# Weight sums of six output projection steps made in the mixer and kept in DRAM, and four instead of three pairs of each column group multiplied by sums

## The chip, the cores and the metric

The kernel runs on one core of one Trainium2 chip. The metric is the device time of one execution in microseconds (us), as the median of several runs. All times of single instructions come from one profiled execution. The engines are called PE (TensorE, matrix products), ACT (ScalarE), DVE (VectorE), POOL (GpSimd) and SP (SyncE, which here only issues transfers).

## The reference, cut to what matters

One layer of a streaming encoder: a gated linear attention mixer, an MLP with squared ReLU, and a last norm, on 256 tokens of width 2048, all in float32.

```python
def _gla_mixer(h, w_in, w_gate_up, b_gate, o_norm, w_out):
    proj = h @ w_in                                   # q, k, v, r and the gate's low rank
    ...                                               # chunked gated attention gives o
    o = o * lax.rsqrt(jnp.mean(o * o, axis=-1, keepdims=True) + EPS) * o_norm
    return (o * jax.nn.silu(r)) @ w_out               # the output projection, 2048 x 2048

def _sq_relu_mlp(h, w_up, w_down):
    a = jax.nn.relu(h @ w_up)
    return (a * a) @ w_down

h = x + _gla_mixer(_rmsnorm(x, gla_norm), ...)
h = h + _sq_relu_mlp(_rmsnorm(h, mlp_norm), w_up, w_down)
return _rmsnorm(h, final_norm)
```

The change touches the output projection, `(o * silu(r)) @ w_out`, and work that is put beside an earlier projection.

## The kernel before

**Precision.** Every float32 operand of a product is split into a high part (a copy in the type fp32r, made by ACT in `copy_hi`, L118) and a low part (the rest, made by DVE, L131). A product is then three: high by high, high by low, low by high. A weight tile goes DRAM to `raw` (six buffers, loaded by SP), from `raw` into a pair of tiles `hi` and `lo` (five buffers each, taken by `slots`), and from there to PE. Buffers rotate: a new tile waits until the last reader of the one five (or six) before it is done. So loads and splits run ahead of PE as far as the buffers let them.

**Order of the program.** The mixer runs first: projections for v (first half), k, q, v (second half, L551 and after), r (two halves), each as sixteen steps of 128 rows of the weight (`natural`, L176, and `turned`, L219). Between two steps `pump` takes one piece of side work (the gate, decays, scores L523, attention) from the queue `side`. Then comes the output projection in four column groups of 512 (`out_group`), then the MLP (L867 and after), whose loads of the up projection follow the last group in SP's stream. A scheduler fixes the order of instructions on every engine when the kernel is built; `issue_after` adds orders by hand.

**The output projection.** A group has eight steps, one for each pair `kp` of 128-row blocks of the weight. A *plain* step splits the 2 x 512 columns of its raw tile and multiplies them in 24 matmuls of 256 columns (four blocks of a 2 x 2 product, three terms, two column halves). A step *by sums* treats the pair as a 2 x 2 block product and does it with seven block products instead of eight, 21 matmuls, at the price of sums of weight blocks and of activation blocks. Its work:

- SP loads the two halves (256 KB each, L743) and POOL adds one block onto another with an accumulating transfer of 128 KB (L744);
- ACT and DVE split the three blocks that need no more sums (768 columns) and PE does three of the products (9 matmuls);
- DVE makes the other sums (`weight_sums`, L604 and L605), ACT copies the high parts (two copies of 512), DVE the low part (L773, 1024 columns), and PE does the other four products (12 matmuls). This second half is `pending`: it comes one step later.

Products by sums of the activation go into two extra banks, `sums_banks` (p16 and p57). After the last step by sums of a group ACT copies them out (L779, L780), DVE combines them (L781 to L784) and adds them to the plain banks into h (L787). The same two banks serve the next group.

**Activations.** `turn` transposes the gated output `on` (in group 0, L627) or finished columns of h (in groups 1 to 3, for the MLP), ACT and DVE split them (L640, L641). For the pairs in `FORMED` the split is `turn_pair`: ACT copies, DVE makes the sums of activation blocks (`form_sums`, L617), ACT and DVE split all eight forms (L618, L619). Before, `FORMED` is (0, 1, 7) and the order of the steps is (3, 0, 2, 1, 4, 7, 5, 6) in every group.

## Time and profile before

| | before |
|---|---|
| median of 3 runs | 1044.37 us (1044.07 to 1044.48) |
| the profiled execution | 1043.33 us, span 1041.5 us |
| mean granted clock of PE | 0.999 |
| PE, DVE, ACT, POOL busy | 99%, 83%, 71%, 11% of the span |
| DMA | 226.79 MB, mean 218 GB/s |

The span is what the profiler saw from the first to the last instruction; the execution's own time holds some 2 us more. A busy share is an average over stages; which engine waits for which is read from the chain of work that ended last and from the rows of single stages.

### The profile page before, as it was taken

The page shows a single profiled execution, that of the slowest core. Times are in us where ns is not written, and L with a number is a line of the kernel's source. Part 1 is how long each engine was busy: PE and PEld are TensorE (multiplying, and loading weights), DVE is VectorE, ACT ScalarE, POOL GpSimd, SP SyncE. Part 2 cuts the span into 40 slices and gives each one's busy share as a digit, 9 for nine tenths or more (in the row PEclk, how much of TensorE's full clock was granted, in tenths as well). Part 3 has the DMA queues.
Part 4 walks back from the last instruction along what each step waited for, and adds up shares of the span by engine and source line. Part 5 has one row for each costly group of instructions (what it writes and reads, how often), then busy time and mean ns, then how long its engine had stood idle before and what let it go on. Part 6 is the DMA issues. An engine that isn't in the chain of part 4 may idle for free.

```text
span 1041.5 us, 23180 instructions
## 1 busy us (share of the span) xinstructions
PE 1033.2 (99%) x9058; PEld 1032.8 (99%) x9058; DVE 865.3 (83%) x1171; ACT 736.9 (71%) x1088; POOL 119.5 (11%) x163
## 2 busy tenths in 40 slices
PE   9999999999999999999999999999999999999997
PEld 9999999999999999999999999999999999999997
DVE  6668654657599876989999999999999999999887
ACT  7685544546477665677778788778778778778685
POOL 0000000010111101111111121111111121111100
PEclk9999999999999999999999999999999999999999
DMA  9957664655667687678887887887888888887772
GB/s 341 338 164 220 189 199 144 181 145 180 194 182 210 206 263 197 175 207 239 224 249 226 230 233 227 233 243 214 253 227 225 245 228 228 237 233 219 234 243 86
DMA packets 119453, 226.79 MB, mean 218 GB/s; under 512 B 10752, under 2 KB 27904, under 8 KB 119216
## 3 DMA queue, kind: packets, MB, share of 16 engines
q1 hardware_dynamic: 100768, 207.46, 63.2%
q0 software_dynamic: 17856, 16.26, 10.3%
q10 hardware_dynamic: 720, 1.60, 0.4%
q8 instruction: 71, 1.16, 0.4%
q14 instruction: 38, 0.31, 0.1%
HBM read 223.17 MB, written 2.10 MB: 216 GB/s over the span
## 4 chain that ended last, share of the span: by engine, by line
PE 99%; issue 0%; ACT 0%; DVE 0%; POOLq 0%; POOL 0%; DVEq 0%
PE up L867 33%; PE acc L867 28%; PE acc L176 19%; PE acc L725 8%; PE acc L219 6%; PE aux L219 2%; PE aux L176 1%; PE aux L627 1%; PE aux L523 1%; PE aux L252 0%; ACT sqf L1206 0%; PE acc L424 0%; DVE hf L1278 0%; POOLq L1315 0%; POOL rf L358 0%
## 5 line engine op out<-in xcount | busy, mean ns | idle before, releaser
L118 ACT CAST hi<-raw 128x512 fp32r<-128x512 f32 (+4 forms) x634 | 512.0, 834 | 234.8 <-PE acc L176 69.0
L131 DVE TENSOR_TENSOR lo<-raw,hi 128x768 fp32r<-128x768 f32 (+3 forms) x226 | 238.0, 1057 | 100.1 <-ACT hi L118 97.4
L867 PE MATMUL acc<-hi,act 128*128 128x256 f32 x1696 | 247.7, 276 | 0.0
L867 PE MATMUL up<-hh,hi 128*128 128x256 f32 x1024 | 238.7, 276 | 0.0
L867 PE MATMUL up<-hl,hi 128*128 128x256 f32 x1024 | 238.7, 276 | 0.0
L165 DVE TENSOR_TENSOR lo<-raw,hi 128x1024 fp32r<-128x1024 f32 x160 | 194.7, 1219 | 28.3 <-ACT hi L118 26.3
L867 PEld LDWEIGHTS acc<-hi,act 128*128 128x128 f32 x1696 | 217.6, 188 | 0.0
L867 PEld LDWEIGHTS up<-hl,hi 128*128 128x128 f32 x1024 | 192.2, 188 | 0.0
L867 PEld LDWEIGHTS up<-hh,hi 128*128 128x128 f32 x1024 | 192.2, 188 | 0.0
L1077 POOL DMA_DIRECT2D raw<-in_w_down x112 | 97.1, 867 | 516.1 <-DMA raw<-in_w_down 231.0
L1137 DVE TENSOR_TENSOR lo<-raw,hi 128x1024 fp32r<-128x1024 f32 x112 | 136.4, 1218 | 1.1 <-ACT hi L118 1.1
L867 PE MATMUL up<-hh,lo 128*128 128x256 f32 x1024 | 137.0, 276 | 0.0
L867 PE MATMUL acc<-lo,act 128*128 128x256 f32 x848 | 133.8, 276 | 0.0
L867 PEld LDWEIGHTS up<-hh,lo 128*128 128x128 f32 x1024 | 125.7, 188 | 0.0
L867 PEld LDWEIGHTS acc<-lo,act 128*128 128x128 f32 x848 | 113.4, 188 | 0.0
L176 PE MATMUL acc<-hi,xA 128*128 128x256 f32 (+1 forms) x736 | 105.6, 278 | 0.0
L176 PEld LDWEIGHTS acc<-hi,xA 128*128 128x128 f32 x736 | 94.4, 188 | 0.0
L605 DVE TENSOR_TENSOR raw<-raw 128x512 f32<-128x512 f32 x124 | 85.6, 690 | 3.2
L176 PE MATMUL acc<-lo,xA 128*128 128x256 f32 (+1 forms) x368 | 61.5, 278 | 0.0
L604 DVE TENSOR_TENSOR raw<-raw 128x256 f32<-128x256 f32 x124 | 52.4, 423 | 2.9
L176 PEld LDWEIGHTS acc<-lo,xA 128*128 128x128 f32 x368 | 50.8, 188 | 0.2 <-DVE lo L131 0.2
L219 PE MATMUL acc<-xA,hi 128*128 128x256 f32 x288 | 49.2, 276 | 0.0
(181 smaller groups left out, 1220.0 us busy)
## 6 DMA issues: line engine op xcount, KB each, us to landing
raw<-in_w_up SPq DMA_DIRECT2D x128, 512.0 KB, 4.6
raw<-in_w_down SPq DMA_DIRECT2D x224, 256.0 KB, 4.3
raw<-in_w_in SPq DMA_DIRECT2D x80, 512.0 KB, 3.8
raw<-in_w_down POOLq DMA_DIRECT2D x112, 128.0 KB, 5.0
raw<-in_w_out SPq DMA_DIRECT2D x20, 512.0 KB, 4.9
raw<-in_w_down SPq DMA_DIRECT2D x16, 512.0 KB, 5.0
raw<-in_w_vg SPq DMA_DIRECT2D x14, 520.0 KB, 8.1
raw<-in_w_out SPq DMA_DIRECT2D x24, 256.0 KB, 3.5
```

Of the source, the lines that this page charges most:

```text
L118: last_hi[0] = nc.scalar.copy(to, raw)
L131: last_lo[0] = nc.vector.tensor_tensor(lo[:, s], raw[:, s], hi[:, s].bitcast(F32), op=ALU.subtract)
L165: last_lo[0] = nc.vector.tensor_tensor(to[1], dst, to[0].bitcast(F32), op=ALU.subtract)
L176: nc.tensor.matmul(o[:, m], x, w[:, m], start=first and c == 0, stop=last, skip_group_check=True)
L219: nc.tensor.matmul(o, u[:, i, s], m, start=kt == 0 and n == 0 and j % 2 == 0, stop=kt == KT - 1 and n == 2, skip_group_check=True,)
L523: nc.tensor.matmul(o, kab[:, k[0], c0 + c, k[1] : k[1] + P], q(qt[:, c0 + c]), start=c == 0, stop=c == 1)
L604: nc.vector.tensor_tensor(u[:, 2], u[:, 0], u[:, 2], op=ALU.subtract)
L605: return nc.vector.tensor_tensor(u[:, 1::2], u[:, 1::2], u[:, 2:3].to_broadcast([P, 2, T]), op=ALU.subtract)
L725: newest[0] = nc.tensor.matmul(bank[:, o + d : o + d + T], x, w[:, d : d + T], start=bank in sums_banks and bank.name not in begun, stop=l ...
L867: newest[0] = nc.tensor.matmul(o, x, w, start=first, stop=last, skip_group_check=True).ins
L1077: nc.gpsimd.dma_start(out=raw[:, :T], in_=src[:, 0, T:], accum_op=ALU.add)
L1137: last_lo[0] = nc.vector.tensor_tensor(to[1][:, :G], u, to[0][:, :G].bitcast(F32), op=ALU.subtract)
```

## The change

Six steps of the output projection, pairs 1 and 6 in column groups 1, 2 and 3, get the sums of their weights made ahead. `make_sums` gives two jobs for each: `high` takes a raw tile and a pair of high/low tiles, loads the 512 KB of the pair (SP), makes all sums on DVE (three instructions: a block added, then the two of `weight_sums`), copies the high part (ACT) and stores it to a tile in DRAM (POOL's queue); `low` makes the low part (DVE) and stores it too. `pump` now takes one job after its side work; the jobs come in threes (high, low, nothing), eighteen in all, from the second v projection on.

In the output projection such a step loads 128 + 256 KB of raw weights for its first half, and both made parts (2 x 512 KB) into a half of a new tile `pre`, all on SP's queue; it has no accumulating transfer, no `weight_sums` and no split in its second half. `pre` lies in the buffer that `on` had, and its two halves alternate.

With that, pair 6 joins `FORMED` in all groups: sixteen steps by sums for twelve. In group 0 all four are made as before, and the order is (3, 0, 2, 1, 4, 7, 6, 5); in groups 1 to 3 it is (1, 3, 7, 2, 0, 6, 4, 5), with two steps made ahead and two made as before. The transposes of h move from the second to the third step there.

```diff
@@ -76,6 +76,7 @@
     tmp = ctx.enter_context(tc.tile_pool(name="tmp", bufs=2))
     st = ctx.enter_context(tc.tile_pool(name="st", bufs=3))
     psum = ctx.enter_context(tc.tile_pool(name="psum", bufs=1, space=bass.MemoryType.PSUM))
+    dram = ctx.enter_context(tc.tile_pool(name="dram", bufs=1, space=bass.MemoryType.DRAM))
 
     acc_free, aux_free = deque(range(6)), deque([6, 7])
 
@@ -91,7 +92,7 @@
         return psum_bank(aux_free[-1], "aux")
 
 
-    side = deque()
+    side, jobs = deque(), deque()
 
     def pump(n=1):
 
@@ -99,6 +100,8 @@
             for _ in range(n):
                 if side:
                     side.popleft()()
+            if jobs:
+                jobs.popleft()()
 
     def flush():
         while side:
@@ -224,6 +227,44 @@
                     pump()
         return acc
 
+    def weight_sums(u):
+        nc.vector.tensor_tensor(u[:, 2], u[:, 0], u[:, 2], op=ALU.subtract)
+        return nc.vector.tensor_tensor(u[:, 1::2], u[:, 1::2], u[:, 2:3].to_broadcast([P, 2, T]), op=ALU.subtract)
+
+
+    MADE_OUT = ((1, 1), (1, 6), (2, 1), (2, 6), (3, 1), (3, 6))
+    MADE_DOWN = ()
+    made = {}
+
+    def make_sums(key, src):
+
+        made[key] = dram.tile([2, P, G], F32, tag=f"made{len(made)}", name="made")
+        raw, to = [], []
+
+        def high():
+            raw.append(raw_tile()[:, :G])
+            with tc.issue_after(last_load[0].ins):
+                last_load[0] = nc.sync.dma_start(out=raw[0].rearrange("p (i c) -> p i c", i=2), in_=src)
+            u = raw[0].rearrange("p (f s) -> p f s", f=4)
+            nc.vector.tensor_tensor(u[:, 0], u[:, 0], u[:, 1], op=ALU.add)
+            weight_sums(u)
+            to.extend(slots())
+            nc.scalar.copy(to[0][:, :G], raw[0])
+            nc.gpsimd.dma_start(out=made[key][0], in_=to[0][:, :G].bitcast(F32))
+
+        def low():
+            nc.vector.tensor_tensor(to[1][:, :G], raw[0], to[0][:, :G].bitcast(F32), op=ALU.subtract)
+            nc.gpsimd.dma_start(out=made[key][1], in_=to[1][:, :G].bitcast(F32))
+
+        return high, low
+
+    def make_all():
+        pair = lambda w, c0, g: w[c0 : c0 + 2 * P, g * GT : (g + 1) * GT].rearrange("(i p) c -> p i c", p=P)
+        todo = [make_sums((None, g, kp), pair(w_out, 2 * kp * P, g)) for g, kp in MADE_OUT]
+        todo += [make_sums((ROUNDS - 1, g, kp), pair(w_down, (ROUNDS - 1) * MR + 2 * kp * P, g)) for g, kp in MADE_DOWN]
+        for high, low in todo:
+            jobs.extend([high, low, lambda: None])
+
     HALF = [(0, 512), (512, 1024)]
 
     def even_at(a, b):
@@ -551,6 +592,7 @@
     side.extend([nothing] * 4 + [lambda: two_scores(0), nothing, lambda: two_scores(2)])
 
 
+    make_all()
     acc = natural(row_x, rows(w_in, 3 * KEYW), G, HALF, order=even_at(9, 11))
     flush()
     for t in range(NT):
@@ -600,17 +642,13 @@
         tt(f[:, S2 : S1 + 1], f[:, A22 : A22 + 1].to_broadcast([P, 2, P]), f[:, 0::7], ALU.add)
         tt(f[:, S4], f[:, A12], f[:, S2], ALU.subtract)
 
-    def weight_sums(u):
-        nc.vector.tensor_tensor(u[:, 2], u[:, 0], u[:, 2], op=ALU.subtract)
-        return nc.vector.tensor_tensor(u[:, 1::2], u[:, 1::2], u[:, 2:3].to_broadcast([P, 2, T]), op=ALU.subtract)
-
-    FORMED = (0, 1, 7)
+    FORMED = (0, 1, 6, 7)
     in_forms = lambda a: a.rearrange("p (f s) -> p f s", f=8)
     raw_forms = [in_forms(some[:, 4:6].rearrange("p a b -> p (a b)")), in_forms(mid.tile([P, G], F32, tag="db", name="form"))]
 
     def turn_pair(kp, bank, gain, to):
 
-        raw_form = raw_forms[kp == 1]
+        raw_form = raw_forms[kp % 2]
         for i in range(2):
             s = bank[:, i * T : (i + 1) * T].rearrange("p (t s) -> p t s", t=NT)
             nc.scalar.activation(raw_form[:, A12 + 1 - i :: 2], s, AF.Copy, scale=gain(2 * kp + i))
@@ -652,7 +690,8 @@
     def forms_o(kp):
         if kp < 2:
             return [of_pairs[:, kp, i] for i in range(2)]
-        return [a[:, OFF : OFF + G].rearrange("p (f s) -> p f s", f=8) for a in (oth, otl)]
+        c = (12 * T + OFF + 128, OFF)[kp - 6]
+        return [in_forms(a[:, c : c + G]) for a in (oth, otl)]
 
     def place_o(kt):
 
@@ -710,6 +749,8 @@
             yield
         last_mm[0] = newest[0]
 
+    made_o = []
+
     def out_group(g, order, summed, between):
 
         tt = nc.vector.tensor_tensor
@@ -736,9 +777,20 @@
 
         for step, kp in enumerate(order):
             by = kp in summed
+            ready = made.get((None, g, kp))
             raw = raw_tile()[:, : 2 * GT]
             src = w_out[2 * kp * P : 2 * (kp + 1) * P, g * GT : (g + 1) * GT].rearrange("(i p) c -> p i c", p=P)
-            if by:
+            if ready is not None:
+                if not made_o:
+                    made_o.extend(big.tile([P, 4 * G + 64], F32R, tag="C", name="pre")[:, : 4 * G].rearrange("p (b i c) -> b p i c", b=2, i=2))
+                ready_in = made_o[0]
+                made_o.reverse()
+                last_load[0] = nc.sync.dma_start(out=raw[:, T:GT], in_=src[:, 0, T:])
+                last_load[0] = nc.sync.dma_start(out=raw[:, GT:], in_=src[:, 1])
+                for i in range(2):
+                    last_load[0] = nc.sync.dma_start(out=ready_in[:, i].bitcast(F32), in_=ready[i])
+                ready = [ready_in[:, i] for i in range(2)]
+            elif by:
                 for i in range(2):
                     last_load[0] = nc.sync.dma_start(out=raw[:, i * GT : (i + 1) * GT], in_=src[:, i])
                 nc.gpsimd.dma_start(out=raw[:, :T], in_=src[:, 0, T:], accum_op=ALU.add)
@@ -753,8 +805,9 @@
                 p16, p57 = sums_banks
                 products([(p16, 0, at(A11), block(1)), (banks[0], T, at(A12), block(3)), (banks[0], 0, at(S4), block(2))], w)
                 u = raw.rearrange("p (f s) -> p f s", f=4)
-                with tc.issue_after(last_lo[0].ins):
-                    weight_sums(u)
+                if not ready:
+                    with tc.issue_after(last_lo[0].ins):
+                        weight_sums(u)
             else:
                 for t, i in ((0, 0), (0, 1), (1, 0), (1, 1)):
                     products([(banks[t], 0, row_o(2 * kp + i, t), block(2 * i, 2))], w, step == len(order) - 1 and i == 1)
@@ -765,12 +818,13 @@
                 with tc.issue_after(last_hi[0].ins), tc.issue_after(last_lo[0].ins), then_mm():
                     between[step]()
             if by:
-                def pending(u=raw, at=at, final=kp == [k for k in order if k in summed][-1]):
-                    to = slots()
-                    for a in range(2):
-                        copy_hi(*(x.rearrange("p (f s) -> p f s", f=4)[:, a::2] for x in (to[0][:, :G], u)))
-                    with tc.issue_after(last_lo[0].ins):
-                        last_lo[0] = tt(to[1][:, :G], u, to[0][:, :G].bitcast(F32), op=ALU.subtract)
+                def pending(u=raw, at=at, final=kp == [k for k in order if k in summed][-1], to=ready):
+                    if not to:
+                        to = slots()
+                        for a in range(2):
+                            copy_hi(*(x.rearrange("p (f s) -> p f s", f=4)[:, a::2] for x in (to[0][:, :G], u)))
+                        with tc.issue_after(last_lo[0].ins):
+                            last_lo[0] = tt(to[1][:, :G], u, to[0][:, :G].bitcast(F32), op=ALU.subtract)
                     products([
                         (p57, 0, at(S1), block(0)), (p16, T, at(S2), block(2)),
                         (p57, T, at(S3), block(1)), (banks[1], T, at(A22), block(3)),
@@ -791,18 +845,18 @@
             sq = tmp.tile([P, GT], F32, tag="t512", name="sq", bufs=1)
             nc.scalar.activation(sq, h[:, t, g * GT : (g + 1) * GT], AF.Square, accum_out=hs[:, t, g : g + 1])
 
-    ORDER = (3, 0, 2, 1, 4, 7, 5, 6)
+    ORDER = (3, 0, 2, 1, 4, 7, 6, 5), (1, 3, 7, 2, 0, 6, 4, 5)
     newest[0] = None
     ordered[0] = True
-    out_group(0, ORDER, FORMED, {
+    out_group(0, ORDER[0], FORMED, {
         1: lambda: (turn(on, turned_o, gain_o, 2), turn(on, turned_o, gain_o, 3, forms_o, spare_out(0))),
         3: lambda: begin_out(1),
     })
     hth, htl = (big.tile([P, KT, T], F32R, tag="A" + i, name="h" + i, bufs=1) for i in "hl")
     turned_h = lambda kt: [a[:, kt, :].rearrange("p (t s) -> p t s", t=NT) for a in (hth, htl)]
     for g in range(1, GROUPS):
-        out_group(g, ORDER, FORMED, {
-            1: lambda: turn(h, turned_h, g2, g - 1), 4: lambda: ssq_h(g - 1),
+        out_group(g, ORDER[1], FORMED, {
+            2: lambda: turn(h, turned_h, g2, g - 1), 4: lambda: ssq_h(g - 1),
             **({3: lambda: begin_out(g + 1)} if g + 1 < GROUPS else {}),
         })
     sums = [big.tile([P, 4, T], F32, tag="E" + i, name="sums", bufs=1) for i in "hl"]
```

## The prediction

> **What bounds the kernel now.** I read the page first: its busy times, then its chain.
>
> ```profile
> span 1041.5 us, 23180 instructions
> PE 1033.2 (99%) x9058; PEld 1032.8 (99%) x9058; DVE 865.3 (83%) x1171; ACT 736.9 (71%) x1088; POOL 119.5 (11%) x163
> PE 99%; issue 0%; ACT 0%; DVE 0%; POOLq 0%; POOL 0%; DVEq 0%
> ```
>
> TensorE (PE) is the whole chain. A busy share alone would not prove that it never waits, so I read the chain in order of time, once in the mixer and then through the four column groups of the output projection (start, length, what).
>
> ```profile
> 199.91 2.72 PE acc L176 x24
> ...
> 286.73 3.75 PE acc L725 x33
> 292.23 20.82 PE acc L725 x183
> 313.05 0.87 PE aux L627 x8
> 313.92 20.82 PE acc L725 x183
> ...
> 374.38 1.70 PE up L867 x15
> ```
>
> A step of 24 matmuls of 256 columns takes 2.72 us, 113.3 ns each. A group is 183 matmuls (three steps by sums of 21, five plain ones of 24); 183 x 113.3 ns is 20.74 us against the 20.82 of the chain, and 0.87 us of transposes stand between groups. So in the groups PE waits for at most 0.1 us each: there is nothing to win there but matmuls themselves, and each one left out is worth 113.3 ns as long as its operands come in time. The last row says that the MLP follows at once.
>
> How close the other engines run decides whether they do come in time. The windows view (PE, PEld, DVE, ACT, POOL busy, granted clock, DMA share, GB/s) for group 0, group 1, the mixer's second value projection, the 8.1 us behind it, and the stage in which DMA is full:
>
> ```profile
> 286.60:309.10 22.50, 22.50 (x201) 22.50 (x200) 21.12 (x33) 18.07 (x29) 1.84 (x3) 1.00 0.58 172
> 309.10:330.80 21.70, 21.70 (x193) 21.70 (x193) 20.17 (x28) 16.11 (x27) 3.42 (x4) 1.00 0.74 220
> ...
> 139.60:189.50 49.90, 49.90 (x435) 49.90 (x435) 25.30 (x39) 24.31 (x41) 0.00 (x0) 1.00 0.57 169
> 189.50:197.60 8.10, 8.10 (x74) 8.10 (x73) 6.20 (x8) 4.91 (x7) 0.00 (x0) 1.00 0.50 143
> 18.00:42.00 24.00, 24.00 (x202) 24.00 (x202) 16.25 (x23) 17.05 (x23) 0.00 (x0) 1.00 1.01 382
> ```
>
> In the groups VectorE (DVE) is nearly as full as PE (21.12 of 22.50 us, 20.17 of 21.70); in the mixer it is half idle (25.30 of 49.90). The change uses that: it moves sums from a full stage to an empty one.
>
> **1. Matmuls taken out: 1.36 us.** Sixteen steps of 21 for twelve, the rest of 24: 4 x 3 = 12 fewer matmuls, 12 x 113.3 ns = 1.36 us, all on the path. The built program has just these 12 fewer on PE, and no other change of its kinds of work.
>
> **2. VectorE and ScalarE in the groups.** The prices (count, total, mean ns):
>
> ```profile
> L118 ACT CAST hi<-raw 128x1024 fp32r<-128x1024 f32 x242 | 253.4, 1049 | 125.9 <-PE acc L176 65.6 <-PE acc L219 25.4 <-PE up L867 12.5
> L131 DVE TENSOR_TENSOR lo<-raw,hi 128x768 fp32r<-128x768 f32 x124 | 118.1, 953 | 25.5 <-ACT hi L118 23.8 <-PE up L867 1.4 <-DMA raw<-in_w_down 0.2
> L131 DVE TENSOR_TENSOR lo<-raw,hi 128x1024 fp32r<-128x1024 f32 x82 | 99.9, 1223 | 64.8 <-ACT hi L118 63.9 <-PE acc L725 0.6
> L605 DVE TENSOR_TENSOR raw<-raw 128x512 f32<-128x512 f32 x124 | 85.6, 690 | 3.2
> L604 DVE TENSOR_TENSOR raw<-raw 128x256 f32<-128x256 f32 x124 | 52.4, 423 | 2.9
> L641 DVE SCALAR_TENSOR_TENSOR otl<-aux,colt,oth 128x256 fp32r<-128x256 f32 x10 | 4.4, 477 | 0.0
> ```
>
> A plain step costs DVE 1.22 us; a step by sums 0.95 + 0.42 + 0.69 + 1.22 = 3.28; a step whose sums were made before only the 0.95. Groups 1 to 3 go from five plain and three by sums to four plain, two by sums and two made: 3.28 + 1.22 - 2 x 0.95 = 2.6 us less, so about 17.6 of 21.35 us in group 1. They get easier. Group 0 has none made: it gets a fourth step by sums for a plain one (+2.06), and pair 6 is turned into forms too: sums of 128 and 256 columns (0.28 and 0.42 in the rows below) and a low part, 2 x 0.28 + 0.42 + 1.22 = 2.2 for two splits of 0.48 (+1.25). That is 21.12 + 3.3 = 24.4 us of DVE in a stage of 22.2. The lead must carry 2.2 us, and this is the one place in the groups that I work through instruction by instruction.
>
> DVE overlaps its neighbours a little, so I take distances from start to start:
>
> ```profile
> 292.14 1.26 DVE L641 SCALAR_TENSOR_TENSOR otl<-aux,colt,oth 128x256 fp32r<-128x256 f32 x3
> 293.32 0.28 DVE L617 TENSOR_TENSOR some<-some 128x128 f32<-128x128 f32 x1
> 293.64 1.22 DVE L773 TENSOR_TENSOR lo<-raw,hi 128x1024 fp32r<-128x1024 f32 x1
> 294.79 0.42 DVE L617 TENSOR_TENSOR some<-some 128x256 f32<-128x256 f32 x1
> 295.12 1.26 DVE L641 SCALAR_TENSOR_TENSOR otl<-aux,colt,oth 128x256 fp32r<-128x256 f32 x3
> 296.30 0.28 DVE L617 TENSOR_TENSOR some<-some 128x128 f32<-128x128 f32 x1
> 296.50 2.09 DVE L131 TENSOR_TENSOR lo<-raw,hi 128x768 fp32r<-128x768 f32 x2
> 298.50 0.42 DVE L604 TENSOR_TENSOR raw<-raw 128x256 f32<-128x256 f32 x1
> ...
> 307.97 0.69 DVE L605 TENSOR_TENSOR raw<-raw 128x512 f32<-128x512 f32 x1
> 308.58 0.42 DVE L782 TENSOR_TENSOR some<-some 128x256 f32<-128x256 f32 x1
> ```
>
> That gives 0.39 us for a split of 256 (295.12 to 296.30 for three), 0.20 for 128 columns, 0.33 for 256, 0.61 for 512, 1.00 for 768, 1.15 for 1024. In the changed order DVE has, from 292.14 to the low part of the last step (pair 5): four splits 1.56, four sums of 128 0.80, two of 256 0.66, the low parts of two forms 2.30, two 768 2.00, weight sums 2 x (0.33 + 0.61) = 1.88, three low parts of 1024 3.45; together 12.65, and some 0.5 in which it waits for ScalarE (ACT), which now copies four form halves in a row before it goes on: 305.3. PE has 111 matmuls from 292.23 to that step and reads the low part four later: 292.23 + 115 x 0.1133 = 305.26. It is a draw. The next meeting is the transposes of group 0's h in group 1. DVE adds a low part 1.15, two 768 2.00, two 1024 2.30, weight sums 0.94, the four operations of the final combination 1.32, two adds into h 1.2 and a low part 1.15: 10.1, so 315.4. PE arrives after 111 + 36 matmuls of group 0 and 9 + 24 + 12 + 9 of group 1: 292.23 + 201 x 0.1133 = 315.0. I take 0.4 us of waiting in all; the ends are 0 (ScalarE keeps up, so DVE gains the half microsecond) and 2 us (three or four more waits of that size). The other new neighbour there, the made step that begins group 1 and writes a sums bank which group 0's last products have just left, costs nothing: the built order puts 24 matmuls (2.72 us) between, more than the two ACT copies of that bank pair.
>
> **3. The sums made in the mixer.** Each of the six is a load of 512 KB on SP's queue, 0.42 + 0.42 + 0.69 + 1.22 = 2.76 us of DVE, 1.05 of ACT and two stores of 512 KB from GpSimd's (POOL's) queue. DVE's 16.5 and ACT's 6.3 us fit into idle time of the 58 us (DVE 31.5 busy, ACT 29.2); nothing waits for them on PE directly. The stores stand in POOL's queue before the reciprocal roots of the attention, 0.89 us per issue; those are needed only at the end of the next projection, 16 x 2.72 us. What is left is room: a made pair takes one of the five high/low buffers until its store has landed, and the step after next but two needs that buffer.
>
> ```profile
> 150.72 1.06 ACT L118 CAST hi<-raw 128x1024 fp32r<-128x1024 f32 x1 [1.67 <-PE acc L176]
> 151.81 1.23 DVE L131 TENSOR_TENSOR lo<-raw,hi 128x1024 fp32r<-128x1024 f32 x1 [1.50 <-ACT hi L118]
> ...
> raw<-in_w_in SPq DMA_DIRECT2D x80, 512.0 KB, 3.8
> raw<-in_w_vg SPq DMA_DIRECT2D x14, 520.0 KB, 8.1
> raw<-in_w_out POOLq DMA_DIRECT2D x12, 128.0 KB, 5.2
> out<-hf SPq DMA_DIRECT2D x5, 256.0 KB, 2.6
> ...
> L744 POOL DMA_DIRECT2D raw<-in_w_out x12 | 10.7, 889 | 117.1 <-DMA raw<-in_w_out 69.0 <-DVE some L617 12.6 <-DVE hl L641 9.1
> ```
>
> ACT waits there for PE to free a buffer: the splits run as far ahead as five buffers let them. One made pair comes every three steps, 8.16 us. From a step's low part through the made low part (1.22 + 1.22), POOL's issue (0.89) and the landing L until the next step may use the buffer is 3.33 + L; against 8.16 the splits slip by L - 4.83 per made pair. The margin: a split started at 150.72 and done at 153.04 is for the step that PE begins four steps after the buffer came free, 4 x 2.72 - 2.4 = 8.4 us of lead; one buffer less takes 2.72 and the sums ahead of it 1.5, which leaves 4. The two bursts of scores lend PE 3 us of other work each: 10 us in all, used up by five slips at L = 6.8. No row shows a store of 512 KB from POOL beside loads. The nearest are the store of 256 KB (2.6), a load of this size (3.8), POOL's own accumulating loads (5.2) and, at full DMA, 8.1. I take 5.2, POOL's queue: five slips of 0.4, hidden. The DMA is not full: 9.6 MB of loads (169 x 49.9 + 143 x 8.1) and 9.4 MB made in 58 us is 328 GB/s, against 382 in the stage where it is full.
>
> Here a page speaks against the change. The Trainium skill, DMA: Bandwidth & Descriptors (Anatomy of one DMA), says that a transfer from GpSimd's queue has some 2 us of fixed cost, most of it the receipt of the last write, and that this "can cause a surprisingly long delay especially when the write target is HBM"; its fit gives an estimated 3.2 us for 512 KB. The trace agrees for the one store it has (2.6 us, the fit gives 2.6), not for POOL's 128 KB (5.2, the fit 2.3). By 3.2 nothing slips and the sum is unchanged.
>
> **4. Loads in the groups.** Groups 1 to 3 load 2 x 1.05 MB of made parts and half tiles instead of whole ones: 4 x 0.52 + 2 x 0.66 + 2 x 1.44 = 6.3 MB in 21.35 us, 295 GB/s against 220 before and 382 at full. The first made loads wait for the buffer of the gated output, free when the transposes that read it end at 292.2.
>
> ```profile
> 291.64 1.06 SPq L743 DMA_DIRECT2D raw<-in_w_out  x2
> ```
>
> At 291.64 SP issues the loads of group 1's second step, eight steps ahead of PE; the made loads stand right behind these in the changed order, so SP hardly waits, and eight steps hide it. I take nothing; bounds 0 to 1 us.
>
> **The sum.** -1.36 + 0.4 = -0.96 us. The profiled execution took 1043.33 us for a span of 1041.5, and would take 1042.4; the median of three runs is 1044.37, 0.1% above, so the forecast is 1044.37 - 0.96 = 1043.4.
>
> **Rivals.** *The gain is eaten in group 0.* If DVE comes 0.6 to 3 us later than worked out, PE waits at the two meetings and the time is 1044.0 to 1046.4. For it: the draw above, with no lead left. Against it: the built order already lets the scarce operand through first. *The stores hold the buffers.* At L = 8.1, as loads took at full DMA, five slips of 3.27 less 10 us leave 6.3 us of PE waiting in the mixer: 1043.4 + 6.3 = 1049.7. It is slower than before from L = 7.0 on and by over 0.2% from 7.4. For it: 328 of 382 GB/s, and stores never tried here. Against it: only one row in four is above 5.2. *More than the matmuls.* To gain over 2.1 us, hidden waits in the groups would have to go; the chain leaves some 0.1 us a group. Near impossible.
>
> **How the numbers follow.** Forecast (1042.9 to 1044.0) 0.62, eaten gain (1044.0 to 1046.4) 0.18, stores (above) 0.16, more than the matmuls 0.04. Within 0.2% (2.1 us, about what a measurement can tell from no change) lie the first two: 0.80; slower 0.16, faster 0.04. A range of 1042.6 to 1046.4 holds them. The likeliest case is thus a true gain of 0.1% that counts as no change.
>
> **What would show it.** PE with 12 fewer matmuls and groups 1 to 3 some 0.34 us shorter each, DVE near 17.6 us in them; in group 0 DVE without idle time from 292 to 315 and PE gaps under half a microsecond before pair 5 and before the transposes. Stores that land in 4 to 6 us. Wrong: gaps in PE's chain between 150 and 197 us, ACT there waiting for stores instead of PE, or a group longer than 21.7 us.

## The result, and the profile after

The change makes the kernel slower, by 0.27%: 1046.68 us (1044.15 to 1048.43) against 1043.82 us (1043.21 to 1044.48) before, medians of 20 runs each; the ratio is 1.0027, with a 95% interval of 1.0021 to 1.0033. The forecast was 1043.4 in a range of 1042.6 to 1046.4, so the time lies outside it. The runs of the changed kernel also scatter over 4.3 us, those of the kernel before over 1.3.

The profiled execution of the changed kernel took 1048.16 us, 1.5 us above the median of its twenty runs, and that of the kernel before 1043.33, 0.5 us below its own; so the account that follows is of 4.8 us, not of the 2.9 us between the medians. Page, first lines (span; busy time of each engine; shares of the chain):

```profile
span 1046.3 us, 23261 instructions
PE 1036.5 (99%) x9046; PEld 1035.6 (99%) x9046; DVE 875.2 (84%) x1191; ACT 740.1 (71%) x1091; POOL 124.6 (12%) x173
PE 97%; issue 1%; DMA 1%; DVE 0%; ACT 0%; SPq 0%; POOLq 0%; POOL 0%; DVEq 0%; ACTq 0%
```

PE runs 12 matmuls fewer and is busy 3.3 us longer. The busy share says nothing of it; the chain in order of time does (start, length, what), here from the last scores (L564) to the MLP:

```profile
174.05 2.19 PE aux L564 x16
176.25 2.67 PE acc L179 x23
178.92 0.89 PE aux L564 x8
179.81 8.61 PE acc L179 x73
...
222.09 2.83 PE acc L179 x24
224.92 1.41 PE aux L179 x12
226.33 28.27 PE acc L179 x240
...
291.78 3.75 PE acc L766 x33
295.53 1.75 PE aux L665 x16
297.27 23.26 PE acc L766 x201
320.53 0.94 PE aux L665 x8
321.47 20.48 PE acc L766 x180
...
378.53 11.56 PE up L921 x102
```

The row of 240 matmuls tells most. Before, the same work was one row too:

```profile
222.35 27.20 PE acc L176 x240
```

27.20 / 240 is 113.3 ns for a matmul, 28.27 / 240 is 117.8. PE waits in neither row, the granted clock is 1.00 in both, and the other engines and the DMA do as much beside the one as beside the other. The windows view of the two rows, before and after (length; busy time of PE, PEld, DVE, ACT and POOL; granted clock, DMA share, GB/s):

```profile
222.35:249.55 27.20, 27.20 (x242) 27.20 (x242) 15.33 (x16) 13.73 (x16) 0.55 (x1) 1.00 0.58 169
226.33:254.60 28.27, 28.27 (x243) 28.27 (x242) 15.34 (x16) 13.84 (x16) 0.55 (x1) 1.00 0.56 164
```

So PE has two paces for a stream of 256-column matmuls, and the changed kernel ran nearly the whole first half of r at the slow one: 2.83 us for a step of 24 instead of 2.72. From here on they are called the fast pace (113.3 ns from start to start) and the slow pace (117.8).

By stages, after minus before, from the starts of these rows: 1.18 us until the second v projection starts (139.80 to 140.98; the first loads of the program; kernels of both kinds differ there by as much), **3.87 us in the mixer** (offset 5.05 at the start of group 0, 286.73 to 291.78), **-0.90 us in the groups** (offset 4.15 at the start of the MLP, 374.38 to 378.53), nothing in the MLP, and 0.65 us behind the last matmul. To compare kernels without the first and the last of these, the table at the end of the experiments takes the time from the first matmul of the k projection to the end of the last matmul: 985.22 us before, 988.19 after, 2.97 more.

In the mixer PE has one wait that this view lists, and it is short. The waits view for PE, and for DVE in that stretch (engine, line, what it waited for: total, times, longest):

```profile
PE acc L179 <- DVE vl L429: 0.8, 1, 0.8
```

```profile
DVE lo L134 <- DMA made<-lo: 7.2, 2, 4.6
```

The DMA issues (count, size, median us from issue to landing) and the windows view of the changed kernel and of the one before (the last two columns are DMA share and GB/s):

```profile
made<-hi POOLq DMA_DIRECT2D x6, 512.0 KB, 5.0
made<-lo POOLq DMA_DIRECT2D x6, 512.0 KB, 7.2
```

```profile
149.50:169.50 20.00, 20.00 (x175) 20.00 (x175) 15.27 (x21) 10.47 (x14) 2.44 (x5) 1.00 0.99 342
```

```profile
149.50:169.50 20.00, 20.00 (x175) 20.00 (x174) 10.14 (x15) 8.78 (x14) 0.00 (x0) 1.00 0.66 200
```

The DMA is full in this stretch (0.99 at 342 GB/s), and the stores of the low parts land after 7.2 us in the median. The longest takes 9.2 us, from 175.7 to 184.9 us; in that time the DMA share is 0.84, at 294 GB/s. The timeline of DVE shows what that does:

```profile
185.11 1.23 DVE L134 TENSOR_TENSOR lo<-raw,hi 128x1024 fp32r<-128x1024 f32 x1 [4.64 <-DMA made<-lo]
...
190.48 1.23 DVE L134 TENSOR_TENSOR lo<-raw,hi 128x1024 fp32r<-128x1024 f32 x1 [1.78 <-ACT hi L121]
191.62 1.22 DVE L256 TENSOR_TENSOR lo<-raw,hi 128x1024 fp32r<-128x1024 f32 x1
192.75 1.22 DVE L134 TENSOR_TENSOR lo<-raw,hi 128x1024 fp32r<-128x1024 f32 x1
194.01 0.75 DVE L429 SCALAR_TENSOR_TENSOR vl<-acc,r,vh 128x512 fp32r<-128x512 f32 x1
```

DVE waits 4.64 us for a low buffer that this longest store holds. What follows comes late, with the sixth made pair's low part (L256) among it, and at its end the eviction of the second v projection (L429), whose bank PE needs for r. PE's matmuls around this wait, from the trace's records (start in us, ns since the start before, tile read):

```
193.643  114  acc<-hi,xA
193.756  113  acc<-hi,xA
194.813 1057  acc<-hi,xA     the wait for vl
195.040  227  acc<-hi,xA
195.160  120  acc<-lo,xA
195.278  118  acc<-lo,xA
195.395  117  acc<-hi,xA     ... and nearly all 117 to 119 for the next 59 us
```

Slow stretches that the kernel before does not have: 179.8 to 191.1 us (behind scores that the built order split in two), 194.8 to 254.6 (all but the start of the first r half), 310.2 to 320.4 (end of group 0). The second holds 506 matmuls: 506 x 4.45 ns = 2.3 us. The first holds about 100, 0.4 us. With the wait (1057 - 113 ns = 0.9 us) that is 3.6 of the mixer's 3.87 us.

### The profile page after: what moved, and what is told of

Same layout as the page of the kernel before. It is cut to its first block, busy times and chain, and to the rows that moved or that the text cites. A ratio compares the mean times of both kernels' runs of the same rounds, so it can differ in the third digit from the quotient of the medians.

```text
span 1046.3 us, 23261 instructions
## 1 busy us (share of the span) xinstructions
PE 1036.5 (99%) x9046; PEld 1035.6 (99%) x9046; DVE 875.2 (84%) x1191; ACT 740.1 (71%) x1091; POOL 124.6 (12%) x173
## 4 chain that ended last, share of the span: by engine, by line
PE 97%; issue 1%; DMA 1%; DVE 0%; ACT 0%; SPq 0%; POOLq 0%; POOL 0%; DVEq 0%; ACTq 0%
PE up L921 33%; PE acc L921 28%; PE acc L179 18%; PE acc L766 8%; PE acc L222 6%; PE aux L222 2%; PE aux L179 1%; PE aux L665 1%; DMA raw<-in_w_vg 1%; PE aux L564 1%; DVE lo L134 0%; ACT hi L121 0%; SPq L171 0%; ACT sqf L1260 0%; SPq L354 0%
## 5 line engine op out<-in xcount | busy, mean ns | idle before, releaser
L121 ACT CAST hi<-raw 128x768 fp32r<-128x768 f32 (+4 forms) x630 | 507.5, 834 | 216.2 <-DVE raw L231 59.6
L179 PE MATMUL acc<-hi,xA 128*128 128x256 f32 (+1 forms) x736 | 108.4, 281 | 0.8 <-DVE vl L429 0.8
L232 DVE TENSOR_TENSOR raw<-raw 128x512 f32<-128x512 f32 x128 | 88.4, 690 | 3.4
```

The costliest lines, as they stand in the source:

```text
L121: last_hi[0] = nc.scalar.copy(to, raw)
L179: nc.tensor.matmul(o[:, m], x, w[:, m], start=first and c == 0, stop=last, skip_group_check=True)
L232: return nc.vector.tensor_tensor(u[:, 1::2], u[:, 1::2], u[:, 2:3].to_broadcast([P, 2, T]), op=ALU.subtract)
```

## The experiments

**A word on the code.** `xe` (in tile `xe_gt`) is a second copy of blocks 5 and 6 of x, at another address. In `natural` the argument `order=even_at(a, b)` says at which step of the stage these two blocks come; in the r halves block 5 reads the copy for the first 128 tokens, twelve matmuls. In the kernel before, such a step stands right behind both bursts of scores and behind the transposes of the second r half, and in the groups pair 2 stands behind the transposes; each time the step's first matmuls take 116 to 121 ns, and those behind it 113.

### Where it is lost: mixer alone, projection alone

```diff
-            ready = made.get((None, g, kp))     # mixer alone: FORMED, orders and turns as before
+            ready = None
```

> All six pairs are made and stored in the mixer as in the changed kernel, but nobody reads them: the output projection is that of the kernel before (twelve steps by sums, all made in place, old orders). If what was lost lies in the mixer alone, by 3.9 us in the profiled execution of the changed kernel, this is 1043.8 + 3.9 less what single runs differ, so 1046.5 to 1047.8. If the loss came from the loads and orders of the output projection, it is 1043.8. Pace theory: TensorE runs its 256-column matmuls at 113.3 ns from start to start, and after an interruption at 118 ns, until twelve matmuls on the operand tile xe_gt (or on pair 2 in the groups) bring it back; then the trace has matmuls at 118 ns from the last scores to the end of the first r half, and groups at 113.3. Buffer theory (a store holds a high/low pair): gaps in TensorE, at 113.3 ns otherwise.

1046.74 us against 1044.01, ratio 1.0024 (1.0013 to 1.0035). The whole loss is in the mixer. Its chain:

```profile
224.47 28.27 PE acc L179 x240
```

The slow pace again, from 193.1 to 252.5, and here with hardly a wait: the waits view has no row for PE, and the records show one matmul that starts 222 ns behind the one ahead of it instead of 113 (the view leaves out gaps as short as this). An interruption of 0.11 us was followed by 59.4 us at the slow pace, 2.3 us.

```diff
-        for high, low in todo:
+        made.update({key: made[None, 1, 1] for key in made})
+        for high, low in todo[:1]:              # projection alone: one pair made, read by all six steps
```

> Only the first of the six pairs is made in the mixer, beside the first steps of the second value projection, far from the scores; all six steps of the output projection that use made parts load this one, so the loads and the arithmetic of the groups are those of the changed kernel with other weights in them. Pace theory: nothing is late at the scores nor at the start of r, the mixer takes what it took before, and the groups keep their 0.9 us: 1042.9, with 0.4 us of 118-ns pace at the end of group 0. If each made pair costs its share (3.9 / 6), 1043.5. If the groups were what costs, 1046 or more.

1043.73 us against 1044.01, ratio 0.9995 (0.9986 to 1.0004). The mixer is as before; the groups win 0.15 us instead of 0.9, since in this run PE waits 1.0 us at the transposes of group 0's h for DVE. That is the second meeting of the prediction.

### Whether the pace is a thing of its own

```diff
+    def extra():
+        b = aux_bank()
+        for _ in range(8):
+            nc.tensor.transpose(b[:, :P], ident, ident)
-    side.extend([lambda: None] + [... attend ...])
+    side.extend([lambda: None, extra] + [... attend ...])      # in the kernel before
```

> The kernel before, with eight transposes of 128 x 128 into a bank that nobody reads, put behind the second step of the first r half; nothing waits for them and no other work is added. By their own length they cost 8 x 109 ns = 0.87 us: 1044.9. Pace theory: TensorE goes on at 118 ns instead of 113.3 until the next xe_gt step, which is some 50 us later in the second r half: 4% of 48 us, 2.0 us more: 1046.9.

1047.05 us against 1043.98, ratio 1.0029 (1.0018 to 1.0040). Eight transposes that take 0.87 us cost 3.1.

```profile
195.31 0.87 PE aux L584 x8
196.18 2.83 PE acc L176 x24
...
227.28 25.44 PE acc L176 x216
```

The next three kernels have the same transposes and differ from this one, and from each other, only in the step at which block 5 comes in this stage: `even_at(0, 6)` above, then (2, 6), (3, 6) and (5, 6).

> The kernel before with the eight extra transposes in the first r half, and the xe_gt step third there, so that its twelve matmuls follow the transposes at once. In the run with that step sixth the pace did not come back (120 ns in the xe_gt matmuls, 118 behind them). Pace theory, refined: the xe_gt step brings 113.3 ns back when it meets the phase in which an interruption leaves TensorE, as it does everywhere in the kernel where it stands right behind one: 0.87 + 12 x 7 ns and some 0.2 us, so 1045.1, 1.9 us under the run with the step first (1047.05). If the step has nothing to do with it: 1047.

1044.60 us against 1043.91, 2.4 us under the run with block 5 first. The chain:

```profile
195.12 0.87 PE aux L584 x8
196.00 2.79 PE acc L176 x24
198.78 0.68 PE aux L176 x6
199.46 2.72 PE acc L176 x24
...
225.98 24.49 PE acc L176 x216
```

One step of 2.79, then 2.72 again. From the k projection to the last matmul it takes 986.09 us, 0.87 more than the kernel before: exactly the transposes. So a slow pace was worth 2.1 us here, and the place of one step decides on it.

> The same, with the xe_gt step fourth, one step of 24 matmuls and 12 of the attention behind the transposes. If the phase decides, the pace either comes back there, as in the changed kernel with the step fourth (1045.3), or not, as with the step sixth (1047): this run only adds a point to that.

> The same eight transposes in the kernel before, but the step that reads xe_gt comes sixth in this stage instead of first, behind the transposes. Every engine has the same work as in the run without this shift. Pace theory: the twelve xe_gt matmuls bring 113.3 ns back some 5 to 10 us behind the transposes: 0.87 + about 0.4, so 1045.3, and 1.5 us under the run with the xe_gt step first. If the steps' order does not matter: equal to that run.

1046.88 and 1047.02 us: as with block 5 first. The twelve xe_gt matmuls ran, and behind them the pace was 118 ns as ahead of them. Right behind an interruption the copy works in every place seen. Further behind, it fails in these two runs; it works in the changed kernel with block 5 fourth, below, and at the start of r, 12 us behind the split scores, in the changed kernel (113 ns from 192.5 us on) and in the other five kernels that split them and have block 5 first. That it depends on how PE's stream lies when the step comes is a guess, and why an operand at another address does this is not shown.

### What interrupts PE in the mixer

```diff
-            nc.gpsimd.dma_start(out=made[key][0], in_=to[0][:, :G].bitcast(F32))
-            nc.gpsimd.dma_start(out=made[key][1], in_=to[1][:, :G].bitcast(F32))    # in mixer alone
```

> The mixer-alone kernel without its twelve stores: the six pairs are loaded and their sums and both parts made on VectorE and ScalarE as there, and kept nowhere; the output projection is that of the kernel before. If the stores cause the lateness at the start of r (a low buffer held until its store has landed, 3.7 us of waiting on VectorE in the mixer-alone kernel), the wait and the slow pace behind it go: 1044.0 to 1044.6 (the 12 us at 118 ns behind the last scores may stay). If the added work on VectorE and ScalarE causes it, it stays: 1046.7.

1045.35 us against 1043.98, ratio 1.0013 (1.0004 to 1.0022). The r half runs at the fast pace again:

```profile
223.71 27.20 PE acc L179 x240
```

With all the added work of DVE and ACT and without the stores, the eviction is in time. This run takes away the stores' traffic together with the buffers that they hold; it does not tell the two apart. What stays from the k projection to the last matmul is 0.44 us: 13 us of slow pace behind the split scores. The time was above the expected range by 0.7 us; in the profiled execution 0.9 us lie ahead of the k projection and 0.6 behind the last matmul, compared with the kernel before.

```diff
+            jobs.extend([lambda: None] * (10 if n == 5 else 0) + [high, low, lambda: None])
```

> The changed kernel with the sixth pair made ten steps later, in the middle of the first r half, so that its low part no longer stands ahead of the eviction of the second value projection on VectorE. Pace theory: no wait at the start of r and no slow pace behind it, 0.8 + 2.4 = 3.2 us less than the profiled changed kernel, so about 1043.6 to 1044; 12 us at 118 ns behind the last scores and 10 us in group 0 stay. If six stores in all cost room, wherever they are, 1046 to 1047.

1044.36 us against 1044.01, ratio 1.0002 (0.9994 to 1.0011). Moving one made pair out of the way of the eviction gives back 2.3 us of the median, 3.5 from the k projection to the last matmul (984.69). The two slow stretches that should stay do stay (178.8 to 190.1 and 305.9 to 316.0).

```diff
-    acc = natural(once_x, rows(w_in, 4 * KEYW), G, HALF, order=even_at(0, 6))
+    acc = natural(once_x, rows(w_in, 4 * KEYW), G, HALF, order=even_at(3, 6))    # in the changed kernel
```

> The changed kernel with one number changed: in the first r half the step that reads the second copy of x (xe_gt) comes fourth instead of first. Nothing changes on any engine but the order of the steps. Pace theory: the wait of 0.8 us for the eviction stays, but the twelve xe_gt matmuls now come behind it and bring the pace back to 113.3 ns for the rest of the stage: of some 60 us at 118 ns about 50 are saved 4%, 2.0 us, so 2 us under the changed kernel, about 1044.7. Buffer theory, or a pace set by which buffers the operands lie in: as the changed kernel, 1046.7.

1047.16 us against 1044.01: nothing gained. The copy did bring the fast pace back at 202.8 us, but 1.3 us later PE was interrupted again, by DVE once more, which had just waited 3.95 us for a stored low part:

```profile
203.71 0.62 PE L179 MATMUL acc<-hi,xA 128*128 128x256 f32 x4
204.76 0.50 PE L179 MATMUL aux<-vh,at 128*128 128x256 f32 x2 [0.44 <-DVE on L621]
```

The slow pace then lasted until 253.4. Two of the eight runs took 1044.6 us; no trace shows these.

```diff
-            nc.vector.tensor_tensor(to[1][:, :G], raw[0], to[0]..., op=ALU.subtract)
+            nc.vector.tensor_tensor(raw[0], raw[0], to[0]..., op=ALU.subtract)     # and store raw[0]
```

> The changed kernel, but the low part of a made pair is written over its raw tile and stored from there, so that no low buffer waits for a store; the raw tile (one of six) is held instead. Buffer theory: VectorE no longer waits for stored low parts (7 us in the changed kernel), the eviction at the start of r is in time, and 0.8 + 2.4 us come back: 1043.6 to 1044.2. If VectorE's own added work makes the eviction late, 1046.7.

1049.82 us against 1043.98: worse, though only 0.7 us of DVE's waiting for stores is left. The high buffers are held as well, and now the waiting is there:

```profile
ACT hi L121 <- DMA made<-hi: 12.5, 3, 6.6
...
PE acc L179 <- DVE vl L429: 4.1, 1, 4.1
```

So it was not the low buffers in particular. PE stood still for 4.4 us, and then ran at half its clock for 5 us and more; behind that it was at the fast pace:

```profile
193.90:199.00 5.10, 1.01 (x9) 0.82 (x8) 2.15 (x3) 3.24 (x5) 0.00 (x0) 0.91 0.42 161
199.00:204.00 5.00, 5.00 (x24) 5.00 (x25) 4.25 (x7) 2.88 (x5) 0.56 (x1) 0.50 0.95 246
```

### A version without the interruptions

```diff
-        for high, low in todo:
-            jobs.extend([high, low, lambda: None])
+        for (high, low), at in zip(todo, (0, 3, 6, 24, 33, 37)):
+            jobs.extend([lambda: None] * (at - len(jobs)) + [high, low])
```

> The same spread of the six made pairs, with all sixteen steps by sums as in the changed kernel. The mixer loses nothing; group 0 still has VectorE without lead at its end, which cost 0.4 us as 10 us of slow pace (changed kernel) or 1.0 us as a wait (projection-alone run): 1044.0 - 1.36 + 0.4 to 1.0 = 1043.0 to 1043.6.

1045.10 us against 1043.91, ratio 1.0010 (1.0001 to 1.0019): missed, by 1.5 us. The mixer loses nothing. Group 0 does: PE waits there, and takes the slow pace for 11 us.

```profile
PE acc L766 <- DVE lo L827: 0.8, 1, 0.8
```

DVE had waited 4.1 us for a raw tile of the output projection. POOL issues the first of its accumulating loads at 277.9 us, instead of 273.5 in the changed kernel and 268.4 in the one before. It does not stand behind the stores of the pair that is now made at 263 us, the last of which is issued at 266.9: the timeline has POOL wait for the raw load that it adds onto. Why that load is late was not tried.

> Two edits to the changed kernel. Three pairs are made in the second value projection, well ahead of the scores, and three in the two r halves, where neither scores nor the eviction are due; and group 0 takes three of its pairs by sums instead of four (pair 6 as a plain step, from its forms), as before the change, so fifteen steps by sums in all. Theory so far (stores that land late hold buffers, VectorE is late, TensorE waits and then keeps the slow pace): no wait and no stretch at 118 ns in the mixer, none in group 0: 9 matmuls fewer, 1.02 us, so 1043.0. If made pairs cost wherever they are: 1044 or more.

The second edit is `out_group(0, (3, 0, 2, 1, 4, 7, 5, 6), (0, 1, 7), ...)`. 1043.73 us against 1043.91, ratio 0.9999 (0.9990 to 1.0008). From the k projection to the last matmul it takes 984.20 us, 1.02 less than before: just the nine matmuls.

```profile
292.71 23.20 PE acc L766 x204
315.92 0.87 PE aux L665 x8
316.79 20.48 PE acc L766 x180
```

But of this second, 0.9 us went behind the last matmul: the span ends 8.2 us after it, not 7.25.

### The end of the execution

In all kernels with made pairs the span ends 7.4 to 8.2 us behind PE's last matmul, in the kernel before and those built on it 7.2 to 7.4. Three theories for it, each with a run or two. First, the tiles in DRAM are there:

> The kernel before, with the six tiles in DRAM of the changed one (1 MB each) and one store of 64 KB to each from POOL's queue ahead of the second value projection; nothing else. If the tiles in DRAM make the last output transfers land later, the span ends 7.5 to 8 us behind TensorE's last matmul instead of 7.2, and the time is 1044.2 to 1044.7; if the jobs do it, 7.2 us and 1043.9.

> The run without stores once more (jobs of loads and sums in the mixer, projection of the kernel before), now without the tiles in DRAM, which nothing used there. If the tiles make the end late, the span ends 7.2 us behind the last matmul and the time is 0.5 us under the 1045.35 of that run; if the jobs or the program's length do it, 7.8 us and 1045.3.

7.3 us with the tiles alone (1044.53 us; in the profiled execution its first loads are late by 1.1 us), 7.9 with the jobs and no tiles (1045.26): it is not the tiles. Second, the turn of the eight transfer counters, shifted with loads of 2 KB on SP's queue:

> The spread version with three pairs by sums in group 0, with three loads of 2 KB into a spare tile put ahead of the second r half on SP's queue: it then issues 24 transfers more than the kernel before, a multiple of eight, so that the output transfers use the same counters as there. The order on the other engines is the same. If the turn of the counters makes the end late, the span ends 7.2 us behind the last matmul instead of 8.2 and the whole gain of the groups shows: 1043.9 - 1.0 = 1042.9. If not: 1043.7, as without the loads.

> The kernel before with six such loads of 2 KB at the same place: its output transfers get the counters that those of the changed kernel have. If the turn decides, the span ends 7.6 to 8 us behind the last matmul and the time is 1044.3 to 1044.6; if not, 7.2 us and 1043.9.

8.1 us (1043.80) and 7.4 us (1043.90): it is not the counters, or hardly. Third, instruction blocks that are loaded among the last output transfers. In the trace's list of transfers nine of the kernels so far have an 8 KB packet of the instruction queue 1.4 to 4.3 us behind the last matmul; their last output data came 5.68 to 6.20 us behind it, in the nine others after 5.55 to 5.77. The packet comes when ScalarE has some 1730 instructions in the trace and VectorE some 1980; the kernel before ends with 1722 and 1953.

> The spread version with three pairs by sums in group 0, and thirty copies of one column each on ScalarE and on VectorE added in the second half of the first r half, where both have idle time. The instruction blocks that were loaded during the last output transfers are then loaded some thirty instructions earlier, 10 to 15 us ahead of the end. If these loads make the end late: the span ends 7.2 to 7.3 us behind the last matmul, and the gain of the groups shows, 1043.9 - 1.0 = 1042.9. If not: 1043.7 to 1043.8, as in the spread version.

> The kernel before with twelve such copies on ScalarE and thirty on VectorE in the first r half: the two instruction counts end where those of the changed kernel end (about 1735 and 1985), and nothing else changes. If the instruction loads make the end late: 7.7 to 8 us behind the last matmul, 1044.4 to 1044.7. If not: 7.2 us and 1043.9.

The blocks moved as meant: in the first run they are loaded 17.8 and 11.9 us ahead of the last matmul's end, in the second one is loaded 2.0 us behind it. The last output data came 5.77 us behind the last matmul instead of 6.05 in the spread version, and 5.79 instead of 5.62 in the kernel before; the span ended 7.9 us (from 8.2) and 7.4 us (from 7.25) behind it. That would put 0.2 to 0.3 us down to these loads. But the kernel before with six small loads has no such packet there, and its last data (5.77 us) and its end (7.4 us) come just as late as with the small copies; so even this part is not shown, and the late end stays open. The first run, 1043.40 us (1042.94 to 1043.73) against 1043.85 (1043.32 to 1044.33), is the lowest of all, but the interval of its ratio (0.9987 to 1.0005) holds 1: no version was shown to beat the kernel before.

### All runs

Medians in us, beside those of the kernel before taken with them; from the first matmul of the k projection to the end of the last matmul; and from there to the end of the span.

```
kernel                        median   before   k proj. to last   behind it
before                                 1043.82      985.22          7.25
the changed kernel           1046.68   1043.82      988.19          7.90
mixer alone                  1046.74   1044.01      988.03          7.56
projection alone             1043.73   1044.01      985.07          7.36
changed, block 5 fourth      1047.16   1044.01      988.09          7.88
changed, sixth pair later    1044.36   1044.01      984.69          8.01
mixer alone, no stores       1045.35   1043.98      985.66          7.81
before + transposes          1047.05   1043.98      988.23          7.23
 the same, block 5 third     1044.60   1043.91      986.09          7.25
 the same, block 5 fourth    1046.88   1043.91      988.18          7.26
 the same, block 5 sixth     1047.02   1043.98      988.18          7.24
changed, low part in place   1049.82   1043.98      991.85          7.39
spread, sixteen by sums      1045.10   1043.91      985.77          7.90
spread, fifteen by sums      1043.73   1043.91      984.20          8.19
 the same + 3 small loads    1043.80   1043.94      984.19          8.11
 the same + 30 small copies  1043.40   1043.85      984.19          7.89
before + DRAM tiles          1044.53   1043.90      985.25          7.29
no stores, no DRAM tiles     1045.26   1043.90      985.66          7.88
before + 6 small loads       1043.90   1043.94      985.19          7.43
before + small copies        1044.03   1043.85      985.21          7.44
```

## Why the prediction was wrong

**What bounds the kernel** was right, and so was the worth of a matmul, 113.3 ns, as long as the pace is the fast one. That PE has another was not seen, though the trace of before shows it for half a step behind every burst of transposes, and through the first v projection.

**Part 1** (1.36 us of matmuls) was right: 20.48 us for 180 matmuls in groups 1 to 3 against 20.82 for 183, and -1.02 us for nine matmuls in the spread version.

**Part 2** was right in size and wrong in kind. The draw at the low part of pair 5 was met: PE waited there, but for some 20 ns, and then ran 10 us at the slow pace, 0.48 us (23.26 for 201 matmuls is 115.7 ns each). In other runs the same shortage shows as a wait of 1.0 us (projection alone). The forecast had 0.4 us, so the sum for the groups (-0.96, measured -0.90) came out near by a term of another kind. DVE in group 1 was forecast at 17.6 of 21.35 us and is busy 18.7 (in group 2, 17.1).

**Part 3** is where the prediction failed, at three of its steps.
- "The DMA is not full: ... 328 GB/s, against 382": it was full at 342 for 20 us. The figure of 382 came from a stage of loads alone. That the stores lower the rate is not shown: from 169.5 to 175.7 us, with stores under way too, the DMA moved 399 GB/s at a share of 1.01.
- "I take 5.2 ...: five slips of 0.4, hidden": the stores of low parts landed after 7.2 us, just above the point of 7.0 from which the rival *the stores hold the buffers* was to decide. Its mechanism came true: DVE and ACT waited for stores, two of the signs that the prediction named came (a gap in PE's chain at 193.8 us, ACT waiting 1.3 us for a store), and without the stores the wait is gone. Its price did not: at 7.2 its own formula gives five slips of 2.37 less 10, 1.9 us of waiting (6.3 at 8.1), and PE waited 0.9 us.
- "Nothing waits for them on PE directly" and the whole sum priced a wait by its length. The term that is missing is the pace: a wait of 0.9 us (of 0.1 in the mixer alone) set PE to 117.8 ns for 60 us, 2.3 us, and scores split in two did so for 12 us, 0.4. Eight transposes in the kernel before show it with nothing else changed: 0.87 us of work, 3.0 us of time.

The estimate from the Trainium skill, DMA: Bandwidth & Descriptors (Anatomy of one DMA), 3.2 us for such a store, would have been further off: 5.0 (high parts) and 7.2 (low parts) were measured beside the loads. The store of 2.6 us that had agreed with it was one of SP's queue.

**Part 4** held: the loads of made parts landed after 6.5 us and PE did not wait for them; the rate in group 1 was 307 GB/s, estimated at 295.

**The rest.** The sum started from 1044.37 us, a median of three runs; twenty give 1043.82, so 0.55 us of the forecast was its base, and the same sum from there gives 1042.9. The 0.65 us behind the last matmul were in no step, and their cause is open. The size of the loss in single runs may depend on whether an interruption falls into the r half at all, which would explain the scatter of the runs; only one execution of each kernel has a trace, so this is not shown.

## What to carry to other kernels

Where one engine runs a long even stream, do not price an interruption by its length: read the distance between its instructions ahead of it and behind it, since a stall of 0.1 us can leave the stream 4% slower until something brings it back. A busy share of 99%, an empty waits view and a full clock do not rule that out; length divided by count in the chain's rows does. And transfers added to a stage must be priced with all of its traffic: a rate at which the DMA was full in another stage (382 GB/s) is no bound, since here it was full at 342.

## What the hardware showed that was not expected

- PE's two paces for float32r matmuls of 256 columns, 113.3 and 117.8 ns from start to start, both at a granted clock of 1.00, each kept for tens of microseconds. The Trainium skill, TensorE: Matmul & The Clock Gate (Back-to-back issue gap), has a formula for the gap of a single isolated matmul that gives an estimated 109.2 ns for 256 columns; no matmul of 256 columns here shows that figure in a stream.
- What ends the slow pace: twelve matmuls on an operand at another address, right behind the interruption (2.1 us saved by the place of one step; further behind, not every time).
- A standstill of 4.4 us halved PE's clock, for 6.8 us by the trace's record of the granted clock. The Trainium skill, TensorE: Matmul & The Clock Gate (Part 1: The HAM clock gate), says that an idle window of some 3.4 us does this. The trace agrees, and the shorter waits here, up to 1.0 us, left the clock at 1.00.
- Stores of 512 KB from POOL's queue beside loads: 5.0 and 7.2 us (medians), with the DMA full at 342 GB/s in a stretch of 20 us.
- Instructions are loaded during the execution as DMA packets, of 8 KB in one queue (41 packets, 0.34 MB, on the page of the changed kernel), some of them among the last output transfers. That they make the end later is not shown.
